# A tile of its own for each evicted query-key piece, and the staging of meta values on the tiles of the head outputs

## The chip, the cores and the metric

One core of one Trainium2 chip. The metric is the device time of one execution in microseconds (us). Instructions run on five engines, each in the order of its own program: TensorE (PE, with its weight loads as PEld), VectorE (DVE), ScalarE (ACT), GpSimd (POOL) and SyncE (SP), which issues most transfers (DMA). An engine that waits holds up all that stands behind it in its own program.

## The reference

One block of a streaming encoder, for 16 meta tokens and 1024 frames of width 1024. Both attention branches take a common input projection; one is softmax attention with a forget term, the other is stick-breaking attention.

```python
xn = rms_norm(h, norm_gains[layer, 0])
proj = xn @ w_in[layer]
q_a, k_a, v_a, f_a, q_b, k_b, v_b, g_a, g_b = jnp.split(proj, SPLIT_POINTS, axis=-1)
log_f = jax.nn.log_sigmoid((f_a + b_forget[layer]).astype(jnp.float32))
o_a = forgetting_attention(_split_heads(q_a, N_HEADS_FOX), ..., log_f.transpose(0, 2, 1))
o_b = stick_breaking_attention(_split_heads(q_b, N_HEADS_SB), ...)
mixed = (jax.nn.sigmoid(g_a) * (o_a @ w_o_fox) + jax.nn.sigmoid(g_b) * (o_b @ w_o_sb)) @ w_out[layer]
h = h + rms_norm(mixed, norm_gains[layer, 1])
xn = rms_norm(h, norm_gains[layer, 2])
u = causal_depthwise_conv(xn @ w_up[layer], conv_w[layer], conv_b[layer])
ffn = (gelu(u_gate) * u_val) @ w_down[layer]
h = h + rms_norm(ffn, norm_gains[layer, 3])
```

The forget branch computes softmax(q k / 8 + c[t] - c[s]), where c is the running sum of log_f. The stick-breaking branch computes sigmoid(z[t,s]) times the product of (1 - sigmoid(z[t,j])) for s < j < t. Eight heads of 64 in each branch, in blocks of 128 queries.

## The kernel before

Every product is made of three: each operand is split into a rounded high part and a low part, and high x high, high x low and low x high are added up in one PSUM bank (`products`, L133). The 1040 token columns are cut into three pieces, PCS = 272, 384 and 384 columns, so that a piece fits a bank.

**The heads.** Heads run as x = 0 to 15: branch b=0 (forget) heads 0 to 7, then b=1 (stick-breaking) heads 0 to 7. For one head, `qk_head` projects q and k together: 24 matmuls for a piece into a "lin" bank of pool `pl` (2 banks, L339 `pq`), evicted by VectorE into `qkt` (L343). ScalarE copies it to the high parts (L345, L347) and GpSimd, or VectorE in b=1 from head 2 on, subtracts the low parts (L90, into q2 and kb). `v_pair` does the values of two heads: `pv` in the same "lin" banks, evicted into `vt` (one buffer, L301), transposed (`vtr`, L309), and split into vv. The 16 meta values are transposed by themselves (`vtm`, L314), copied by ScalarE to a small tile `vst` (L322) and sent to `vmini` by two transfers (L325). The transposes use a bank of pool psS, tag "s", in b=0, and of psT, tag "tr", in b=1.

**Attention.** Scores (L362, L363, with a mask product L365 in b=1) go to psS banks. In b=0 VectorE takes the minimum, ScalarE the exponential, VectorE the reciprocal, and GpSimd multiplies the row (L410, tile `pr`, six buffers). In b=1 ScalarE makes two sigmoids (L395, L396), VectorE a running product (L413, `kp`), GpSimd a product (L414). For each two blocks (c = 0 to 3) there follow transposes of `pr` (`tm`, L424, and `tr`, L434), a cast by ScalarE (L438) and a subtraction by VectorE (L439) into `pt`, and products with the values (`po`, L428 and L444). The lower half of `po` is copied by ScalarE to `ot` (L447, two buffers), added by VectorE into `os` (L449), and sent out.

**Banks.** psS, psT and psO have 3, 2 and 1 banks for b=0. At the end of head 7 they are closed and opened anew with 2, 3 and 1 (`psum_pools`); the new banks wait for the last readers of the old.

**What sets the order.** The program is written head by head: attention of head x, then `prep` of the next head (q, k and, every second head, v), then `gate` (L133 `pg`, evicted at L500). A scheduler in the framework orders the instructions of each engine from a simulated timeline: it puts on each engine what it takes to be ready first, in program order where all are ready, and an eviction under `high_priority` earlier. Projections (`pq`, `pv`, `pg`) so end up between the attention steps, and fill TensorE while the other engines work on a row. Which tile an instruction asks for decides what it must wait for, and with it the order.

In names such as s0772 the digits are the branch, the head, the block and the column piece; po073 is branch, head and pair of blocks, tr0731 one group of it; pq, qkt are branch, head and piece; pv, vt, vtr, vst are branch and pair of heads (with piece or group); pr076 is head and block with a leading branch digit; pg41 is gate and piece. q211 is the second-half query tile of branch 1, head 1; kb1 is one of two key tiles shared by all heads.

Of the kernel before, what the change touches and what calls it, by code (L numbers as in the profile page):

```python
# [8 lines left out]
F32 = mybir.dt.float32  # L9
# [7 lines left out]
P = 128  # L17
D = 1024
KT = 8
NM = 16  # L20
# [5 lines left out]
DH = 64  # L26
# [23 lines left out]
def block_kernel(ctx, tc, xa, xb, wqk, wv, wf, bfg, wg, wo, wout, wup, wdn, gains, conv, cst, out):  # L50
# [124 lines left out]
    with ExitStack() as pa:  # L175
# [100 lines left out]
        for i in range(2):  # L276
            t = ap1.tile([P, 256], F32R, name=f"ptm{i}")
# [12 lines left out]
        def v_pair(b, p):  # L290
            hi, lo = load_w(wv[b * 4 + p], KT * P, f"v{b}{p}", hv=True) if b or p else early["v"]()
            yield
            vt = ap1.tile([P, L], F32, tag="vt", name=f"vt{b}{p}")
            for i, (n0, n1) in enumerate(PCS):
                if b == 0 and p == 0:
                    ps = psT.tile([P, 512], F32, tag="tr", name=f"pv{b}{p}{i}")
                else:
                    ps = pl.tile([P, 512], F32, tag="lin", name=f"pv{b}{p}{i}")
                products(ps[:, : n1 - n0], hi, lo, xs[i], 0, KT, 0, n1 - n0)
                with tc.high_priority(offset=200):  # L300
                    nc.vector.tensor_tensor(vt[:, n0:n1], ps[:, : n1 - n0], rs1[:, n0:n1], op=ALU.mult)  # L301
                yield
            vps, vtag = (psT, "tr") if b else (psS, "s")
            vv = ap2.tile([P, 8, 2, 2, DH], F32R, tag="vv", name=f"vv{b}{p}")
            for g in range(2):
                pt = vps.tile([P, 4, 2, DH], F32, tag=vtag, name=f"vtr{b}{p}{g}")
                for j in range(4):
                    c0 = NM + (4 * g + j) * P
                    nc.tensor.transpose(pt[:, j, :, :].rearrange("p a b -> p (a b)"), vt[:, c0 : c0 + P], ident)  # L309
                hv = vv[:, 4 * g : 4 * g + 4, :, 0, :]  # L310
                nc.scalar.copy(hv, pt)
                nc.vector.tensor_tensor(vv[:, 4 * g : 4 * g + 4, :, 1, :], pt, f(hv), op=ALU.subtract)
            pt = vps.tile([P, 4, 2, DH], F32, tag=vtag, name=f"vtm{b}{p}")
            nc.tensor.transpose(pt[0:NM, 0, :, :].rearrange("p a b -> p (a b)"), vt[:, 0:NM], ident)  # L314
            vm = vms[p % 2]
            src = pt[0:NM, 0, :, :]
            nc.scalar.copy(vm[0:NM, :, 0, :], src)
            nc.scalar.copy(vm[32:48, :, 0, :], src)
            nc.vector.tensor_tensor(vm[0:NM, :, 1, :], src, f(vm[0:NM, :, 0, :]), op=ALU.subtract)
            nc.vector.tensor_tensor(vm[32:48, :, 1, :], src, f(vm[0:NM, :, 0, :]), op=ALU.subtract)  # L320
            st = ap2.tile([NM, 2, DH], F32, tag="vst", bufs=1, name=f"vst{b}{p}")
            nc.scalar.copy(st, src)  # L322
            for hh in range(2):
                h = 2 * p + hh
                nc.sync.dma_start(vmini[b][NM * h : NM * (h + 1), :], st[:, hh, :])  # L325
            yield vv, vm

        def qk_head(b, h):
            hi, lo = load_w(wqk[b * NH + h], KT * P, f"qk{b}{h}", nc.vector if b and h > 1 else None, hv=not (b and h > 1)) if b or h else early["qk"]()
            yield  # L330
            q2 = ap2.tile([P, L], F32R, tag="q2", name=f"q2{b}{h}")
            k1 = ap2.tile([P, L], F32R, tag="k1", name=f"k1{b}{h}")
            k2 = kb[h % 2]
            if b == 1 and h < 2:
                nc.vector.memset(f(k2[DH:P, :]), 0.0)
            low = nc.vector if b and h > 1 else nc.gpsimd
            for i, (n0, n1) in enumerate(PCS):
                ps = pl.tile([P, 512], F32, tag="lin", name=f"pq{b}{h}{i}")
                w = n1 - n0  # L339
                products(ps[:, :w], hi, lo, xs[i], 0, KT, 0, w)  # L340
                t = ap2.tile([P, 384], F32, tag="qkt", name=f"qkt{b}{h}{i}")[:, :w]
                with tc.high_priority(offset=200):
                    nc.vector.scalar_tensor_tensor(t, ps[:, :w], qsc[:, b : b + 1], rs1[:, n0:n1],  # L343
                                                   op0=ALU.mult, op1=ALU.mult)
                nc.scalar.copy(q2[0:DH, n0:n1], t[0:DH])  # L345
                sub(low, q2[DH:P, n0:n1], t[0:DH], q2[0:DH, n0:n1])
                nc.scalar.copy(k1[DH:P, n0:n1], t[DH:P])  # L347
                sub(low, k2[0:DH, n0:n1], t[DH:P], k1[DH:P, n0:n1])
                yield
            nc.sync.dma_start(f(k1[0:DH, :]), f(k1[DH:P, :]))  # L350
            if b == 0:
                if h:
                    nc.sync.dma_start(f(k2[64:66, :]), cd[h])
                q1 = qb[h % 2]
                nc.sync.dma_start(f(q1[0:DH, :]), f(q2[0:DH, :]))
                yield q2, k1, q1[0:66, :], k2[0:66, :]
            else:
                yield q2, k1, q2, k2
# [755 lines left out]
```

## Time and profile before

| | |
|---|---|
| time, median of 3 runs | 1648.77 us (1648.71 to 1649.92) |
| the profiled execution's own time | 1648.93 us |
| its span | 1647.1 us |
| mean clock granted to TensorE | 0.998 |
| TensorE busy | 1623.7 us (99%) |
| VectorE, ScalarE, GpSimd busy | 1096.3, 830.5, 375.5 us |

The span is what the trace covers; 1.8 us of the execution lie around it. The next lines are the page's first engine rows by slices of the span, 40 equal slices of 41 us each, in tenths (9 is 90% or more).

```profile
PE   8999999999999999999999999999999999999997
DVE  7456566666788878655536887888888877333532
ACT  6354445444666766544345554565555556333420
POOL 1365656556243333403201000000000000000001
PEclk9999999999999999999999999999999999999999
```

Attention and its projections fill the slices from the second to about the eighteenth; then come the output projections and the gated merge, the up-projection, the convolution and the down-projection.

### The profile page before, as it was taken

Reading aid. Unit: us, or ns where it says so; the run is one execution under the profiler, and the core shown is the slowest. Engines: PE = TensorE matmul, PEld = TensorE weight load, DVE = VectorE, ACT = ScalarE, POOL = GpSimd, SP = SyncE. Lnnn points to the kernel's source line nnn. Section 1 sums busy time; section 2 is a strip of 40 time slices with the busy share of each in tenths; the row PEclk is TensorE's granted clock in tenths of the full one; section 3 lists DMA queues with packets and bytes.
Section 4 is the critical chain, followed back from the end, with each engine's and each line's share of the span. In section 5 each row is a group of like instructions: output and inputs, shape, how many; then the busy total and the mean of one; then the engine's idle time right before and its main releaser. Section 6 shows DMA issues by size and latency. Waiting matters only on the chain.

```text
span 1647.1 us, 29715 instructions
## 1 busy us (share of the span) xinstructions
PE 1623.7 (99%) x11672; PEld 1572.0 (95%) x11672; DVE 1096.3 (67%) x1874; ACT 830.5 (50%) x1712; POOL 375.5 (23%) x264
## 2 busy tenths in 40 slices
PE   8999999999999999999999999999999999999997
PEld 7999999999999999999999999999999999888887
DVE  7456566666788878655536887888888877333532
ACT  6354445444666766544345554565555556333420
POOL 1365656556243333403201000000000000000001
PEclk9999999999999999999999999999999999999999
DMA  4312121212111111274343552223332236445552
GB/s 183 85 57 72 54 63 51 75 39 72 46 48 41 40 32 62 73 208 146 125 129 114 170 172 85 97 90 108 97 99 97 78 109 204 140 145 150 175 183 77
DMA packets 77788, 168.48 MB, mean 102 GB/s; under 512 B 10288, under 2 KB 33584, under 8 KB 77648
## 3 DMA queue, kind: packets, MB, share of 16 engines
q1 hardware_dynamic: 77104, 166.06, 32.0%
q8 instruction: 92, 1.51, 0.4%
q10 hardware_dynamic: 544, 0.52, 0.1%
q14 instruction: 48, 0.39, 0.1%
HBM read 124.85 MB, written 35.24 MB: 97 GB/s over the span
## 4 chain that ended last, share of the span: by engine, by line
PE 95%; issue 2%; ACT 1%; DVE 1%; DMA 1%; SPq 0%; POOL 0%; DVEq 0%; POOLq 0%; ACTq 0%
PE pd L945 15%; PE A L815 13%; PE pq L133 11%; PE pg L133 10%; PE B L815 7%; PE pm L638 6%; PE pv L133 6%; PE pu L638 5%; PE y L133 5%; PE po L444 4%; PE tr L434 4%; PE R L815 3%; PE s L363 2%; PE s L362 2%; PE tm L424 1%
## 5 line engine op out<-in xcount | busy, mean ns | idle before, releaser
L945 PE MATMUL pd<-g,wh_d 128*128 128x512 f32 x616 | 191.5, 392 | 0.0
L994 POOL TENSOR_TENSOR acc<-acc,hr 128x512 f32<-128x512 f32 x4 | 5.0, 1274 | 720.8 <-DVE acc L987 720.8
L745 DVE SCALAR_TENSOR_TENSOR c<-us,cb,c 128x512 f32<-128x512 f32 x176 | 129.7, 748 | 32.9 <-ACT c L743 31.9
L945 PEld LDWEIGHTS pd<-g,wh_d 128*128 128x128 f32 x616 | 115.3, 188 | 25.0
L410 POOL TENSOR_SCALAR pr<-pr,mx 128x144 f32<-128x144 f32 (+3 forms) x64 | 114.5, 1794 | 106.2 <-DVE mx L409 56.7
L414 POOL TENSOR_TENSOR pr<-pr,kp 128x143 f32<-128x143 f32 (+3 forms) x64 | 84.7, 1328 | 168.1 <-DVE kp L413 106.4
L439 DVE TENSOR_TENSOR pt<-tr,pt 128x512 fp32r<-128x512 f32 (+1 forms) x160 | 98.8, 633 | 33.7 <-ACT pt L438 31.1
L945 PE MATMUL pd<-g,wl_d 128*128 128x512 f32 x308 | 120.8, 392 | 0.0
L444 PE MATMUL po<-pt,vv 128*128 128x256 f32 (+1 forms) x640 | 110.1, 280 | 0.0
L438 ACT CAST pt<-tr 128x512 fp32r<-128x512 f32 (+1 forms) x160 | 83.7, 542 | 51.9 <-PE tr L434 49.3
L90 DVE TENSOR_TENSOR wl_d<-wr_d,wh_d 128x896 fp32r<-128x896 f32 (+1 forms) x42 | 47.7, 1136 | 89.7 <-ACT wh_d L121 89.5
L413 DVE TENSOR_TENSOR_SCAN kp<-kp 128x144 f32<-128x144 f32 (+3 forms) x64 | 95.1, 1492 | 11.9 <-ACT kp L395 11.3
L444 PEld LDWEIGHTS po<-pt,vv 128*128 128x128 f32 x640 | 94.2, 189 | 0.2
L403 ACT ACTIVATE pr<-s,mx 128x144 f32<-128x144 f32 (+6 forms) x112 | 59.7, 539 | 67.2 <-DVE mx L401 52.2
L434 PE MATMUL tr<-cs,pr 128*128 128x128 f32 x576 | 92.7, 274 | 0.0
L121 ACT CAST wh_d<-wr_d 128x896 fp32r<-128x896 f32 (+1 forms) x42 | 41.2, 980 | 88.7 <-PE pd L945 84.0
L743 ACT ACTIVATE c<-us,cb 128x512 f32<-128x512 f32 x88 | 71.0, 815 | 21.1 <-DMA gdr<-c 15.1
L362 PE MATMUL s<-k,q 128*128 128x264 f32 (+9 forms) x240 | 79.2, 332 | 0.0
L133 PE MATMUL pg<-xh,wh_g 128*128 128x384 f32 (+1 forms) x384 | 74.8, 324 | 1.6 <-DVE qkt L343 1.4
L133 PE MATMUL pq<-xh,wh_qk 128*128 128x272 f32 (+1 forms) x360 | 74.5, 327 | 0.0
L133 PE MATMUL y<-o,wh_o 128*128 128x258 f32 x512 | 73.0, 284 | 1.1 <-ACT o L575 0.9
L133 PE MATMUL pg<-xh,wl_g 128*128 128x384 f32 (+1 forms) x384 | 73.9, 322 | 0.0
(300 smaller groups left out, 4484.7 us busy)
## 6 DMA issues: line engine op xcount, KB each, us to landing
wu<-in_wup SPq DMA_DIRECT2D x40, 512.0 KB, 3.6
wr_d<-in_wdn SPq DMA_DIRECT2D x28, 448.0 KB, 3.9
gdr<-c SPq DMA_DIRECT2D x44, 256.0 KB, 3.8
gr<-gdr SPq DMA_DIRECT2D x44, 256.0 KB, 4.2
gs<-gd SPq DMA_DIRECT2D x16, 513.0 KB, 4.2
wr_g<-in_wg SPq DMA_DIRECT2D x16, 512.0 KB, 3.6
wr_wo<-in_wout SPq DMA_DIRECT2D x16, 512.0 KB, 3.4
wr_qk<-in_wqk SPq DMA_DIRECT2D x15, 512.0 KB, 5.1
```

What stands on the lines that cost most here:

```text
L133: marks["mm"] = nc.tensor.matmul(ps, w[:, k * P : (k + 1) * P], x[:, k - k0, n0:n1], start=(k == k0 and s == 0), stop=(k == k1 - 1 and s = ...
L362: nc.tensor.matmul(ps[:tn, :n], q2[:, t0 : t0 + tn], k1[:, s0:s1], start=True, stop=False)
L410: nc.gpsimd.tensor_scalar(pr[:, :w], pr[:, :w], z, None, op0=ALU.mult)
L413: nc.vector.tensor_tensor_scan(r, r, r, 1.0, op0=ALU.mult, op1=ALU.bypass)
L414: nc.gpsimd.tensor_tensor(pr[:, : w - 1], pr[:, : w - 1], kp[:, 1:w], op=ALU.mult)
L434: nc.tensor.transpose(tr[:, x * P : (x + 1) * P], prs[tb][:, NM + j * P : NM + (j + 1) * P], ident)
L439: nc.vector.tensor_tensor(pt[:, 1, :n], tr[:, :n], f(pt[:, 0, :n]), op=ALU.subtract)
L444: nc.tensor.matmul(po[:, o0:256], vj, pt[:, s, 256 * j : min(256 * j + 256, n)], start=False, stop=(last and j == 1 and s == 1))
L638: nc.tensor.matmul(ps, (hi, hi, lo)[s][:, c : c + P], xs[kh][s == 1][:, k, :], start=(s == 0 and kh == 0 and k == 0), stop=(s == 2 and kh ...
L745: nc.vector.scalar_tensor_tensor(c, u[:, :, tap : tap + 256], cb[:, x, tap : tap + 1], c, op0=ALU.mult, op1=ALU.add)
L815: nc.tensor.matmul(ps, w[:, (k0 + i) * P : (k0 + i + 1) * P], x[:, i, :], start=(first and s == 0 and i == 0), stop=(s == 2 and i == 3), s ...
L945: nc.tensor.matmul(ps, a[:, (k - k0) * P : (k - k0 + 1) * P], x[:, c0:c1], start=(k == 0 and s == 0), stop=(k == NK - 1 and s == 2))
```

## The change

It does two things. The eviction tile `qkt` was one tag with two buffers of 384 columns, through which a head's three pieces rotated. Now the first piece has a tag of its own ("qk0", one buffer of 272 columns), and the other two pieces share a tag with two buffers, so that each piece of a head has its own tile. The staging tile `vst` had a buffer of its own in pool ap2. Now it is taken from pool apl under tag "ot", whose two buffers also take the lower halves of the head outputs. Per partition of SBUF the first part takes 1088 bytes more and the second 512 less.

```diff
@@ v_pair
-            st = ap2.tile([NM, 2, DH], F32, tag="vst", bufs=1, name=f"vst{b}{p}")
+            st = apl.tile([NM, 2, DH], F32, tag="ot", name=f"vst{b}{p}")
             nc.scalar.copy(st, src)
@@ qk_head
                 products(ps[:, :w], hi, lo, xs[i], 0, KT, 0, w)
-                t = ap2.tile([P, 384], F32, tag="qkt", name=f"qkt{b}{h}{i}")[:, :w]
+                t = ap2.tile([P, w], F32, tag="qkt" if i else "qk0", bufs=2 if i else 1, name=f"qkt{b}{h}{i}")
```

No instruction is added or removed. The order changes on all engines, from the first head to the end of attention, and is the same from there on. Three places follow.

**TensorE at the border from b=0 to b=1.** From the last scores of head (0,7); pg40 is the first piece of gate 4. Before:

```order
L362 MATMUL s0772_4517<-k107_4089,q207_4088 128x344
L363 MATMUL s0772_4517<-kb1_151,qb1_152 128x344
L133 MATMUL pg40_5296<-xh0_114,wh_g4_5292 128x258 x8
L133 MATMUL pg40_5296<-xl0_115,wh_g4_5292 128x258 x8
L133 MATMUL pg40_5296<-xh0_114,wl_g4_5293 128x258
L444 MATMUL po071_4374<-pt0710_4386,vv03_3578 128x256
L133 MATMUL pg40_5296<-xh0_114,wl_g4_5293 128x258 x5
L444 MATMUL po071_4374<-pt0710_4386,vv03_3578 128x256 x3
L444 MATMUL po071_4374<-pt0711_4397,vv03_3578 128x256
L424 MATMUL tm072_4444<-cs_74,pr074_4409 16x128
L424 MATMUL tm072_4444<-cs_74,pr075_4426 16x128
```

After the change:

```order
L362 MATMUL s0772_4517<-k107_4089,q207_4088 128x344
L363 MATMUL s0772_4517<-kb1_151,qb1_152 128x344
L444 MATMUL po071_4374<-pt0710_4386,vv03_3578 128x256 x4
L444 MATMUL po071_4374<-pt0711_4397,vv03_3578 128x256
L424 MATMUL tm072_4444<-cs_74,pr074_4409 16x128
L424 MATMUL tm072_4444<-cs_74,pr075_4426 16x128
L444 MATMUL po071_4374<-pt0711_4397,vv03_3578 128x256
L444 MATMUL po071_4374<-pt0711_4397,vv03_3578 128x128 x2
L434 MATMUL tr0720_4450<-cs_74,pr074_4409 128x128
L434 MATMUL tr0720_4450<-cs_74,pr075_4426 128x128
L434 MATMUL tr0720_4450<-cs_74,pr074_4409 128x128
L434 MATMUL tr0720_4450<-cs_74,pr075_4426 128x128
```

The projections pg40, pg41, pg42, pv110 and pv111, 120 matmuls, now stand ahead of s0772; from it to the first matmul of pv112 there are only rows of attention and the transposes vtr10 and vtm10.

**GpSimd in the same place.** From the normalisation of block 6 of head (0,7) on (wl_v11 is the low part of a weight tile). Before:

```order
L410 TENSOR_SCALAR pr076_4490<-pr076_4490,mx76_4491 128x912
L90 TENSOR_TENSOR wl_v11_5658<-wr_v11_5655,wh_v11_5657 128x1024
L90 TENSOR_TENSOR q211_5193<-qkt110_5221,q211_5193 64x272
L90 TENSOR_TENSOR kb1_151<-qkt110_5221,k111_5194 64x272
L90 TENSOR_TENSOR q211_5193<-qkt111_5252,q211_5193 64x384
L90 TENSOR_TENSOR kb1_151<-qkt111_5252,k111_5194 64x384
L410 TENSOR_SCALAR pr077_4507<-pr077_4507,mx77_4508 128x1040
L90 TENSOR_TENSOR q211_5193<-qkt112_5283,q211_5193 64x384
L90 TENSOR_TENSOR kb1_151<-qkt112_5283,k111_5194 64x384
```

After the change, from the row behind pr075 on:

```order
L90 TENSOR_TENSOR q211_5193<-qkt110_5221,q211_5193 64x272
L90 TENSOR_TENSOR kb1_151<-qkt110_5221,k111_5194 64x272
L410 TENSOR_SCALAR pr076_4490<-pr076_4490,mx76_4491 128x912
L90 TENSOR_TENSOR q211_5193<-qkt111_5252,q211_5193 64x384
L90 TENSOR_TENSOR kb1_151<-qkt111_5252,k111_5194 64x384
L90 TENSOR_TENSOR q211_5193<-qkt112_5283,q211_5193 64x384
L90 TENSOR_TENSOR kb1_151<-qkt112_5283,k111_5194 64x384
L410 TENSOR_SCALAR pr077_4507<-pr077_4507,mx77_4508 128x1040
L414 TENSOR_TENSOR pr100_4910<-pr100_4910,kp00_4911 128x143
```

wl_v11 has moved up, ahead of pr070, and all six subtractions of head (1,1) now stand ahead of pr077, two of them also ahead of pr076.

**VectorE at the end of head (1,5).** The third eviction of the last head, qkt172; kp57 is the running product over the last block of head 5. Before:

```order
L439 TENSOR_TENSOR pt1522_7285<-tr1522_7281,pt1522_7285 128x384
L90 TENSOR_TENSOR kb1_151<-qkt170_7913,k117_7887 64x272
L90 TENSOR_TENSOR kb1_151<-qkt171_7944,k117_7887 64x384
L90 TENSOR_TENSOR q217_7886<-qkt170_7913,q217_7886 64x272
L413 SCALAR_TENSOR_TENSOR kp57_7313<-kp57_7313 128x1040
L343 SCALAR_TENSOR_TENSOR qkt172_7975<-pq172_7950,qsc_77,rs1_113 128x384
L500 TENSOR_TENSOR gst120_8493<-pg120_8468,rs1_113 128x258
L90 TENSOR_TENSOR q217_7886<-qkt171_7944,q217_7886 64x384
L413 SCALAR_TENSOR_TENSOR kp60_7604<-kp60_7604 128x144
L449 TENSOR_TENSOR os152_7294<-po152_7250,ot152_7292 64x256
L90 TENSOR_TENSOR q217_7886<-qkt172_7975,q217_7886 64x384
```

After the change:

```order
L439 TENSOR_TENSOR pt1521_7274<-tr1521_7269,pt1521_7274 128x512
L343 SCALAR_TENSOR_TENSOR qkt172_7975<-pq172_7950,qsc_77,rs1_113 128x384
L439 TENSOR_TENSOR pt1522_7285<-tr1522_7281,pt1522_7285 128x384
L90 TENSOR_TENSOR kb1_151<-qkt170_7913,k117_7887 64x272
L90 TENSOR_TENSOR kb1_151<-qkt171_7944,k117_7887 64x384
L90 TENSOR_TENSOR kb1_151<-qkt172_7975,k117_7887 64x384
L90 TENSOR_TENSOR q217_7886<-qkt170_7913,q217_7886 64x272
L413 SCALAR_TENSOR_TENSOR kp57_7313<-kp57_7313 128x1040
L90 TENSOR_TENSOR q217_7886<-qkt171_7944,q217_7886 64x384
L90 TENSOR_TENSOR q217_7886<-qkt172_7975,q217_7886 64x384
L413 SCALAR_TENSOR_TENSOR kp60_7604<-kp60_7604 128x144
```

qkt172 has moved from behind kp57 and three subtractions to a place before pt1522, ahead of all of them.

## The prediction

> **What bounds the kernel now.** I read the page first (busy time by engine, then the chain that ended last), then what TensorE waited for, then the time line at each place where the new order differs.
>
> ```profile
> span 1647.1 us, 29715 instructions
> PE 1623.7 (99%) x11672; PEld 1572.0 (95%) x11672; DVE 1096.3 (67%) x1874; ACT 830.5 (50%) x1712; POOL 375.5 (23%) x264
> PE 95%; issue 2%; ACT 1%; DVE 1%; DMA 1%; SPq 0%; POOL 0%; DVEq 0%; POOLq 0%; ACTq 0%
> PE pv L133 <- ACT whi_v L105: 6.7, 2, 5.6
> PE s L363 <- DMA kb<-cd: 1.4, 1, 1.4
> PE pg L133 <- DVE qkt L343: 1.4, 1, 1.4
> PE pv L133 <- DVE vt L301: 0.8, 2, 0.5
> PE vtr L309 <- DVE vt L301: 0.3, 1, 0.3
> ```
>
> TensorE is busy 99% of the span and holds 95% of the chain. It is idle 1647.1 - 1623.7 = 23.4 us, and the longest waits are the first weights (6.7 us), which the change does not touch. So a changed order cannot win more than a few us, but it can lose many: the instruction set is the same in both programs, and whatever idle time the new order makes on TensorE is added to the time in full. The question is where, in the new order, TensorE has only work whose inputs are not there yet.
>
> **What the change removes.** With one tile for each of a head's three pieces, the eviction qkt (L343) no longer waits for the readers of the piece before last. The trace has one TensorE wait of that kind:
>
> ```profile
> 621.70 1.65 PE L133 MATMUL pg<-xh,wh_g 128*128 128x384 f32 x8 [1.37 <-DVE qkt L343]
> 623.20 1.55 PE L133 MATMUL pg<-xl,wh_g 128*128 128x384 f32 x8
> 624.58 1.55 PE L133 MATMUL pg<-xh,wl_g 128*128 128x384 f32 x8
> ```
>
> The third piece of the last head stood behind a scan and three subtractions on VectorE; now it stands ahead of them. The projection bank comes free early, and 1.4 us go (1.37 at most, since 1.37 is all that was waited; nothing else on TensorE waits for that bank in this stretch). Call it -1.4.
>
> The order at the start of attention changes too. The first-head product of s with kb (L363) waits 1.38 us for the forget row, which comes from HBM at the end of a long chain.
>
> ```profile
> 77.05 0.69 PE L363 MATMUL s<-kb,qb 66*128 66x144 f32 x3 [1.38 <-DMA kb<-cd]
> 77.83 1.55 PE L133 MATMUL pv<-xh,wh_v 128*128 128x384 f32 x8
> 79.22 1.55 PE L133 MATMUL pv<-xl,wh_v 128*128 128x384 f32 x8
> ```
>
> Eight matmuls of 384 columns go at 79.22 - 77.83 = 1.39 us, 0.174 each. In the new order 18 more projection matmuls (2 of 272 and 16 of 384 columns, 2 x 0.125 + 16 x 0.174 = 3.0 us) stand before that product, but the forget products that begin the chain stand 9 matmuls later (1.6 us), and a weight cast and an eviction go ahead inside the chain on VectorE (the neighbours of this kind take some 0.6 us each). The wait becomes 1.38 + 1.6 - 3.0 = 0 to 1.2 us; I take 0.4: -1.0 (bounds -1.4 and 0). The 0.3 us of vtr behind vt also goes, because the first vtr moved behind other matmuls: -0.3 (bounds -0.3 and 0).
>
> **What the change moves.** The copy of the meta values (vst, L322) now asks for an "ot" tile, two of which rotate through all head outputs. It therefore comes after the outputs of the head before; in the order on ScalarE vst01 is behind ot013, some 15 rows later.
>
> ```profile
> L322 ACT COPY vst<-vtm x8: 238/255/256, 47.7 to 640.5; 16x128 f32<-16x128 f32 x8
> DMA to landing us min/median/max: 1.7/1.7/1.8
> ```
>
> The copy itself is a quarter of a us, and its two transfers land 1.7 us after they are issued; the output after next (ot021 for vst01) now waits for them, but comes several us later, so I cost that at nothing, and at 1.5 each if the cover were gone. Until vst is done it holds the score bank in which vtm lies (in b=0 that is tag "s"). Scores come later, projections earlier, and this adds up: by head 7 of b=0 its attention stands 18 us of TensorE work later than before, with the projections that used to lie between it already spent. As long as there is work to do that costs nothing. It is given back at one place, the border from b=0 to b=1.
>
> ```profile
> 401.24 0.32 PE L363 MATMUL s<-kb,qb 66*128 66x344 f32 x1
> 401.40 1.11 PE L133 MATMUL pg<-xh,wh_g 128*128 128x258 f32 x8
> 432.78 0.91 PE L133 MATMUL pv<-xh,wh_v 128*128 128x384 f32 x4
> 401.56:432.78 31.22, 31.22 (x230) 30.94 (x228) 21.64 (x37) 20.72 (x50) 16.22 (x14) 1.00 0.21 67
> 13.38 1.85 PE L133 MATMUL pv<-xh,wlo_v 128*128 128x272 f32 x8
> 16.56 1.16 PE L133 MATMUL pq<-xh,wlo_qk 128*128 128x272 f32 x8
> ```
>
> The stretch from the last score of head (0,7) (s0772, ends at 401.56) to the third piece of pv11 (432.78) is 31.22 us, and TensorE (second number) is never idle in it. By the order of before it holds 120 projection matmuls: 24 of 258 columns (0.119 each, since the 8 last 1.11 us in all and the last of them 0.28), 72 of 384 (0.174), and 24 of 272 (0.125, in the same way from the 1.16 of the row at 16.56). That is 2.9 + 12.5 + 3.0 = 18.4 us. The other 12.8 us are attention. In the new order all 120 stand ahead of s0772, and none is left between it and pv112. No other can be put there: pv110 and pv111 hold both projection banks until VectorE evicts them into vt, a single tile still read by vtr10 and vtm10, and those need banks that open when the outputs of head (0,7) are done. So the chain below is bare, with 12.8 us of TensorE work inside it:
>
> ```profile
> 398.60 2.56 POOL L410 TENSOR_SCALAR pr<-pr,mx 128x912 f32<-128x912 f32 x1 [5.28 <-DVE mx L409]
> 401.14 2.40 POOL L90 TENSOR_TENSOR wl_v<-wr_v,wh_v 128x1024 fp32r<-128x1024 f32 x1
> 403.61 0.77 POOL L90 TENSOR_TENSOR q<-qkt,q 64x272 fp32r<-64x272 f32 x1
> 404.46 0.76 POOL L90 TENSOR_TENSOR kb<-qkt,k 64x272 fp32r<-64x272 f32 x1
> 405.30 1.00 POOL L90 TENSOR_TENSOR q<-qkt,q 64x384 fp32r<-64x384 f32 x1
> 407.75 2.92 POOL L410 TENSOR_SCALAR pr<-pr,mx 128x1040 f32<-128x1040 f32 x1 [0.37 <-ACT ot L447]
> 401.44 0.42 ACT L345 CAST q<-qkt 64x272 fp32r<-64x272 f32 x1
> ```
>
> GpSimd. The subtractions into q211 and kb1 write buffers that s0772 reads, so they start when it ends, after ScalarE's first copy (0.42, with a hand-off 0.7). In the new order the last normalisation (pr077, 2.92) comes behind two small ones, pr076 and four larger ones: 0.7 + 0.77 + 0.76 + 2.56 + 4 x 1.00 + 2.92 = 11.7, and six gaps of 0.08 (403.61 + 0.77 to 404.46) make 12.2; I say **12.4**. In before pr077 was done at 410.67, 9.1 us after s0772, under cover.
>
> From there to pv112 the work is transposes, casts, subtractions and products of four rounds, then vtr, vtm, and the eviction of vt. The nearest row is the same passage at the end of head (1,3), almost without idle time:
>
> ```profile
> 556.42 0.27 PE L424 MATMUL tm<-cs,pr 128*16 128x128 f32 x1
> 557.90 1.61 PE L133 MATMUL pv<-xh,wl_v 128*128 128x384 f32 x8
> 565.42 0.81 PE L133 MATMUL pv<-xh,wh_v 128*128 128x384 f32 x3 [0.32 <-DVE vt L301]
> 556.96 1.61 DVE L413 TENSOR_TENSOR_SCAN kp<-kp 128x272 f32<-128x272 f32 x2
> 416.31 0.99 DVE L413 TENSOR_TENSOR_SCAN kp<-kp 128x400 f32<-128x400 f32 x1 [0.16 <-ACT kp L395]
> 421.10 1.25 DVE L413 TENSOR_TENSOR_SCAN kp<-kp 128x528 f32<-128x528 f32 x1
> 424.12 1.52 DVE L413 TENSOR_TENSOR_SCAN kp<-kp 128x656 f32<-128x656 f32 x1 [0.72 <-ACT kp L395]
> 429.54 1.79 DVE L413 TENSOR_TENSOR_SCAN kp<-kp 128x784 f32<-128x784 f32 x1 [3.44 <-ACT kp L395]
> 418.28 0.69 DVE L439 TENSOR_TENSOR pt<-tr,pt 128x512 fp32r<-128x512 f32 x1 [0.20 <-ACT pt L438]
> 431.25 0.39 DVE L449 TENSOR_TENSOR os<-po,ot 64x256 f32<-64x256 f32 x1
> 431.56 0.42 DVE L301 TENSOR_TENSOR vt<-pv,rs 128x272 f32<-128x272 f32 x1
> ```
>
> There, tm133 to pv132 takes 565.42 - 556.42 = 9.0 us. Here VectorE has four scans in the passage (0.99 + 1.25 + 1.52 + 1.79 = 5.55), four subtractions (at most 2.8), and three evictions of about 0.4: 9.5 us, and with four hand-offs of some 0.4 at most 11.2. So pv112 starts 12.4 + 9.0 = 21.4 to 23.6 us after s0772, with 12.8 us of work for it: idle 8.6 to 10.8, I take **+9.7**. The wider bounds are 5 (GpSimd's small pieces done before s0772 and pr077 4 us sooner) and 13 (VectorE and GpSimd in each other's way).
>
> The wait is in order on TensorE, so all later work is late by the same amount; behind pv112 both orders have done the same work, and nothing later waits long enough to hand it back (pv behind vt, 0.8 in all).
>
> At the end of head (1,3) itself eight pv131 matmuls (8 x 0.174 = 1.4) moved from behind tm133 to ahead of it, and scores and transposes of 0.7 moved in: 0.32 of wait becomes 0.32 + 1.4 - 0.7 = 1.0. By the order the score s1420 is also 2.6 us later, so up to two scans (1.61) get in the way. That is +0.7 to +2.3, or less if vt is early: I take **+1.3** (bounds 0.3 and 2.5).
>
> **The sum:** -1.4 - 1.0 - 0.3 + 9.7 + 1.3 = +8.3. The profiled execution took 1648.93 us (1.8 around its span), within 0.2 of the median of 1648.77, so 1648.93 + 8.3 = **1657.2**. With the inner bounds of the terms the sum gives 1655.1 to 1660.6, with the wider ones 1651.1 to 1663.0.
>
> **Rivals.**
> First, **the border is covered** and the time is not slower. If the chain after s0772 took no more than the 12.8 us of attention that lie in it, the order would cost nothing there: -1.4 - 1.0 - 0.3 + 1.3 = -1.4, or 1647.5 (1646.1 without the loss in head (1,3)). Up to a chain of 12.8 + 1.4 + 3.3 = 17.5 the result would still be no difference. For it speaks that TensorE was never idle in the 31.22 us of before; against it that 18.4 of those were projections, that pr077 took 9.1 us even then, and that the passage behind it takes 9.0 where almost nothing is idle. Chance 0.17, with 0.05 of it for a time faster by over 0.2%, which would need gains that no wait here offers.
>
> Second, **TensorE runs slowly after the stall.** At the start eight matmuls of 272 columns lasted 1.85 us, three us later 1.16, so they were slower by 59% without any wait. After the 1.37 us gap at 621.70 the next eight took 1.50 (623.20 - 621.70) and the next 1.38, so such a gap does not do it. If the border made 6 us of work run at the early pace, 6 x 0.59 = 3.5 more: 1660.7. My pieces of idle time are under 2 us each, with work between; chance 0.11. The Trainium skill, "TensorE: Matmul & The Clock Gate", section "What's actually happening", says that the array falls to half its clock after an idle window of about 3.4 us and needs as long a busy one to return; one such window would be an estimated 3.4 us more here, none if the pieces of idle time stay as short as I think. The slow start agrees with that rule; no row shows a fall in mid-run.
>
> Third, **more places lose**: banks and POOL work moved in the earlier heads too, and two to four waits of the size of those above (1.4 to 1.7) would add 3 to 7: 1660 to 1664. The trace has no such wait in b=0 after the first head, and the order leaves projections ahead of every bank there; 0.12.
>
> That **the change does nothing** is out: the evictions' waits are gone in the order, and qkt172 moved ahead of the scan. The forecast has the rest, 0.60.
>
> **How the numbers follow.** What a measurement of this kernel can tell from no change is about 0.2%, 3.3 us, so no difference reaches to 1652.1. Slower: 0.60 + 0.11 + 0.12 = 0.83, less 0.05 for the low end of the forecast (1651.1) = 0.78; same 0.12 + 0.05 = 0.17; faster 0.05. The range must take in the forecast's bounds and the first rival's 1646.1 (cases of 0.17): 1646 to 1664. The upper end is the third rival's. The likeliest case alone has 1651 to 1663.
>
> **What would show it.** Right: a TensorE idle time of 8 to 11 us in all between s0772 and pv112, about 20 us later than the 401 of before, released by transposes' evictions, by pr on GpSimd and, last, by vt on VectorE; pr077 ending some 12 us after s0772; no wait of pg for qkt; less than 1.2 us behind kb<-cd; about 1 us more at pv132. Wrong: TensorE busy in that stretch (first rival), or matmuls of 384 columns at over 0.25 us behind it (second), or idle time of over 1 us in heads 1 to 6 of b=0 (third).

## The result and the profile after

The changed kernel takes **1671.22 us** (median of 4 runs, 1668.63 to 1672.59) against 1648.74 before (4 runs, 1648.54 to 1649.92): ratio 1.0131, 95% interval 1.0118 to 1.0143. It is slower, as forecast, but by 22.5 us and not by 8.3, and outside the range that ended at 1664.

The page of the changed kernel, its span and its busy times, and then what TensorE waited for (engine, line, what it waited on; us in total, times, longest):

```profile
span 1669.8 us, 29694 instructions
PE 1633.4 (98%) x11672; PEld 1577.8 (94%) x11672; DVE 1096.5 (66%) x1874; ACT 829.1 (50%) x1712; POOL 374.2 (22%) x264
PE pv L133 <- ACT whi_v L105: 7.9, 2, 5.7
PE po L444 <- DVE pt L439: 4.5, 7, 1.3
PE pv L133 <- DVE gst L500: 1.8, 1, 1.8
PE po L428 <- DVE ptm L427: 1.8, 3, 0.8
PE po L444 <- ACT pt L438: 1.6, 2, 1.4
PE tr L434 <- DVE ptm L427: 1.4, 1, 1.4
PE pg L133 <- DVE gst L500: 1.4, 1, 1.4
PE pv L133 <- DVE vt L301: 0.9, 1, 0.9
```

The span grew by 22.7 us with the same 11672 matmuls. TensorE's busy time grew by 9.7 (1633.4 less 1623.7), its idle time by 13.0. So part of the loss is waits and part is the same matmuls taking longer. The wait of pg behind qkt (1.37) is gone, as forecast, and so is that of s behind kb<-cd (1.38), of which the forecast left 0.4. In their place stand many waits of the attention products, for the casts and subtractions just ahead of them.

Three stretches of the time line hold most of the loss. The columns are the stretch, its length and, for each engine, busy us and instructions; then TensorE's granted clock, the share of the DMA engines and GB/s. The changed kernel, then the kernel before:

```profile
245.00:260.00 15.00, 12.73 (x78) 11.76 (x77) 7.50 (x20) 10.50 (x27) 10.99 (x8) 0.89 0.17 42
330.00:350.00 20.00, 17.80 (x117) 16.48 (x117) 11.49 (x31) 12.81 (x34) 14.01 (x11) 1.00 0.25 65
425.00:460.00 35.00, 28.90 (x181) 25.89 (x180) 28.29 (x47) 25.06 (x64) 17.73 (x15) 0.90 0.09 18
```

```profile
245.00:260.00 15.00, 15.00 (x108) 14.87 (x107) 9.29 (x27) 6.83 (x23) 5.65 (x5) 1.00 0.13 41
330.00:350.00 20.00, 20.00 (x140) 19.89 (x140) 12.34 (x34) 8.61 (x25) 9.32 (x7) 1.00 0.14 44
425.00:460.00 35.00, 35.00 (x252) 34.46 (x251) 27.54 (x41) 21.82 (x56) 10.63 (x8) 1.00 0.08 24
```

Before, TensorE was busy without a gap in all three. After, it idles 2.3, 2.2 and 6.1 us, and in the first and the third its clock is down. The third is the border that the prediction spoke of. The first two are the ends of heads (0,3) and (0,5), of which it did not.

How late each kernel runs can be read off at equal work. For each matmul I take its start in the trace, less the time that the matmuls ahead of it in its order need at full pace; this lateness, less that of the kernel before at the same amount of work, is what was lost so far. The table gives what was lost in each stretch of work (us), up to 825 us of work, where attention and gates are long over; the four columns on the right are runs told of below. Full pace is read from the usual distance between matmuls of a shape; read a little higher or lower, it moves some tenths of a us between neighbouring rows, and leaves the sums as they are.

| stretch, TensorE work done | forecast | change | change again | pieces only | staging only | hold three |
|---|---|---|---|---|---|---|
| 0 to 225: start, heads (0,0) to (0,2) | -1.3 | +0.7 | -1.3 | -1.0 | -0.1 | +1.8 |
| 225 to 250: end of (0,3) | 0 | +4.5 | +3.4 | -0.2 | 0.0 | +0.8 |
| 300 to 325: end of (0,5) | 0 | +3.7 | +3.7 | 0.0 | -0.1 | 0.0 |
| 375 to 425: border | +9.7 | +12.3 | +12.4 | +6.2 | +3.6 | +1.7 |
| 450 to 475: end of (1,1) | 0 | +1.2 | +1.2 | +1.2 | +0.9 | +1.2 |
| 525 to 550: end of (1,3) | +1.3 | +1.2 | +1.2 | +1.2 | +1.0 | +1.2 |
| 575 to 600: pg behind qkt | -1.4 | -1.7 | -1.7 | -1.7 | -1.3 | -1.7 |
| 675 to 725: last gates, start of the output projection | 0 | +2.6 | +1.0 | +2.2 | -0.2 | +1.6 |
| all the rest | 0 | -1.5 | -1.5 | -1.6 | -0.2 | +1.5 |
| sum | +8.3 | +23.0 | +18.4 | +6.3 | +3.6 | +8.1 |

### The profile page after: what moved, and what is told of

The parts are those of the page before. It is cut to its first block, busy times and chain, and to the rows that moved or that the text cites. A ratio compares the mean times of both kernels' runs of the same rounds, so it can differ in the third digit from the quotient of the medians.

```text
span 1669.8 us, 29694 instructions
## 1 busy us (share of the span) xinstructions
PE 1633.4 (98%) x11672; PEld 1577.8 (94%) x11672; DVE 1096.5 (66%) x1874; ACT 829.1 (50%) x1712; POOL 374.2 (22%) x264
## 4 chain that ended last, share of the span: by engine, by line
PE 91%; DVE 3%; ACT 2%; DMA 2%; issue 1%; POOL 0%; SPq 0%; DVEq 0%; POOLq 0%; ACTq 0%
PE pd L945 15%; PE A L815 13%; PE pq L133 10%; PE pg L133 9%; PE B L815 6%; PE pm L638 6%; PE pv L133 5%; PE pu L638 5%; PE y L133 5%; PE po L444 4%; PE tr L434 3%; PE R L815 3%; PE s L362 2%; PE s L363 2%; DVE kp L413 1%; PE tm L424 1%
## 5 line engine op out<-in xcount | busy, mean ns | idle before, releaser
L444 PE MATMUL po<-pt,vv 128*128 128x256 f32 (+1 forms) x640 | 115.1, 286 | 6.2 <-DVE pt L439 4.5
L133 PE MATMUL pg<-xl,wh_g 128*128 128x384 f32 (+1 forms) x384 | 76.7, 324 | 0.0
```

The costliest lines, as they stand in the source:

```text
L133: marks["mm"] = nc.tensor.matmul(ps, w[:, k * P : (k + 1) * P], x[:, k - k0, n0:n1], start=(k == k0 and s == 0), stop=(k == k1 - 1 and s = ...
L444: nc.tensor.matmul(po[:, o0:256], vj, pt[:, s, 256 * j : min(256 * j + 256, n)], start=False, stop=(last and j == 1 and s == 1))
```

## The border

The changed kernel in the time line of TensorE and of GpSimd: start, us, engine, line, tiles, and in brackets the wait just before:

```profile
428.88 0.32 PE L363 MATMUL s<-kb,qb 66*128 66x344 f32 x1
432.45 0.56 PE L444 MATMUL po<-pt,vv 128*128 128x256 f32 x3 [1.32 <-DVE pt L439]
436.38 0.47 PE L365 MATMUL s<-smask 128*128 128x128 f32 x1 [1.14 <-DVE smask L549]
453.09 1.65 PE L133 MATMUL pv<-xh,wh_v 128*128 128x384 f32 x8 [0.92 <-DVE vt L301]
431.54 2.56 POOL L410 TENSOR_SCALAR pr<-pr,mx 128x912 f32<-128x912 f32 x1
438.49 2.92 POOL L410 TENSOR_SCALAR pr<-pr,mx 128x1040 f32<-128x1040 f32 x1
```

s0772 ends at 429.20, and pr077 is done at 438.49 + 2.92 = 441.41, 12.2 us later (12.4 forecast). pv112 starts at 453.09, 23.9 us after s0772 (21.4 to 23.6 forecast), and waits for vt, as named. With 12.2 us of work in the passage by its order (12.8 in the forecast) it loses 11.7; the term was +9.7.

Two things differ from the forecast. TensorE is idle for only 6.1 us of the passage, where 8 to 11 were named as the sign; the other 5.7 us are its own matmuls taking longer than at full pace, some at half rate (clock 0.50 from 433.3 to 440.1) and some one by one. And no wait for pr is booked on TensorE. Its transpose of pr077 starts at 441.57, 0.16 us after GpSimd is done, right behind work of its own. That work was late as well, behind the mask of the new branch: smask_raw is asked for at 432.90, and its cast on VectorE ends at 436.3 (the wait of 1.14 above). The chain that the profile follows back goes over ScalarE's copies and this load, and not over GpSimd. So two chains end together there, and which of them sets the first half of the passage is not shown.

## The experiments

Four theories. **A**: the loss is projections that run ahead of attention and are then missing, so that attention stands bare. **B**: the pieces part alone makes it; three pieces evicted early put six copies in a row on ScalarE, ahead of the casts. **C**: the staging part alone makes it, by holding a score bank. **D**: the tiles themselves make it, whatever the order.

### One part at a time

Only the pieces (with one tile shared by the two uses of `mini`, which frees 512 bytes per partition; in the run below that has the same sharing, the order on TensorE is that of before up to 619 us):

```diff
-                t = ap2.tile([P, 384], F32, tag="qkt", ...)[:, :w]
+                t = ap2.tile([P, w], F32, tag="qkt" if i else "qk0", bufs=2 if i else 1, ...)
-            w = ap1.tile([2, NH, NM], F32, name=f"mw{b}")
+            w = ap1.tile([2, NH, NM], F32, tag="mw", name=f"mw{b}")
```

> Only the part with a tile for each piece; vst keeps its own buffer (512 bytes per partition come from sharing one small tile between the two uses of mini, which leaves the order as it was). Theory A, projections run ahead of attention and are missing later: in the order of this kernel one bare stretch of attention is left in b=0, 10.8 us of TensorE work at the border (13.8 with both parts; 5.4 and 3.9 more in heads 3 and 5 with both, none of those here), and 7.4 instead of 5.3 in heads (1,1) and (1,3). s0772 to pv112 holds 18.6 us of work here, and the passage took 23.9 with both parts: about 5 us idle at the border, 1 to 3 us in b=1, 1 to 3 in the gates, less 1.4 for pg behind qkt: 1654 to 1660. Theory B, this part alone makes the loss, since three evictions at once set six copies on ScalarE ahead of the casts: 1668 to 1672. Theory C, the vst part makes it: 1646 to 1649.

Only the staging:

```diff
-            st = ap2.tile([NM, 2, DH], F32, tag="vst", bufs=1, name=f"vst{b}{p}")
+            st = apl.tile([NM, 2, DH], F32, tag="ot", name=f"vst{b}{p}")
```

> Only the part with vst on the tiles of the head outputs; qkt as before. Theory A: one bare stretch at the border of 7.1 us, s0772 to pv112 holds 22.5 us of work against a passage of up to 23.9: 0 to 2 us idle there, 1 to 3 in heads (1,1) and (1,3), 0 to 2 in the gates: 1650 to 1655. Theory B (the pieces make the whole loss): 1648 to 1650. Theory C (vst makes it, by holding a score bank): 1668 to 1672.

Measured: pieces alone 1655.00 us (ratio 1.0038, 1.0025 to 1.0052), staging alone 1652.32 (1.0019, 1.0010 to 1.0028), with 1649.06 before. Both lie where A put them; B and C, that one part alone makes the whole loss, fall. The parts are far from adding up: 5.9 and 3.3 us apart, 22.5 together.

Why they don't add up is seen in the passages themselves. At the ends of heads (0,3), (0,5) and (0,7) the chain from the last score of the head to the third piece of the second-next pv is the same kind: casts, subtractions, products, transposes of vt, eviction of vt, with both projection banks held until then. The table gives its length in the trace, and in brackets the TensorE work that the order puts in it (us).

| passage | before | pieces only | staging only | both | both, hold three |
|---|---|---|---|---|---|
| s0372 to pv032 | 21.4 (21.3) | 10.0 (10.1) | 17.6 (17.6) | 7.9 (3.4) | 18.9 (18.7) |
| s0572 to pv102 | 28.9 (28.6) | 10.1 (10.1) | 17.5 (17.5) | 6.5 (3.1) | 29.6 (29.6) |
| s0772 to pv112 | 31.2 (30.7) | 24.5 (18.6) | 25.7 (22.2) | 23.9 (12.2) | 34.3 (32.1) |

At (0,3) and (0,5) a passage takes the work in it or the length of its chain, some 7 us, whichever is longer. At the border it takes some 24 us even with 18.6 or 22.2 us of work in it, since that work does not reach to its end: from the transpose of pr077 to pv112 it takes 11.6 us with the pieces only, 10.5 with the staging only and 11.5 with both. With one part TensorE comes to that transpose 2.3 and 3.3 us after GpSimd is done, so there GpSimd held nothing up. Each part alone uses up 4 to 18 us of the cover and still leaves (0,3) and (0,5) more work than the chain; both together leave 3.4 and 3.1. The end of the border is uncovered by either part alone. The two rows of the time line of TensorE that bound it, pieces only and then staging only:

```profile
412.03 0.32 PE L363 MATMUL s<-kb,qb 66*128 66x344 f32 x1
436.89 0.79 PE L133 MATMUL pv<-xh,wh_v 128*128 128x384 f32 x3 [0.78 <-DVE vt L301]
```

```profile
410.59 0.32 PE L363 MATMUL s<-kb,qb 66*128 66x344 f32 x1
436.64 0.62 PE L133 MATMUL pv<-xh,wh_v 128*128 128x384 f32 x2 [0.78 <-DVE vt L301]
```

What B named is real as part of the chain. At the end of (0,3) in the changed kernel ScalarE does six copies in a row before the cast that TensorE waits for:

```profile
248.47 0.42 ACT L345 CAST q<-qkt 64x272 fp32r<-64x272 f32 x1
248.91 0.42 ACT L347 CAST k<-qkt 64x272 fp32r<-64x272 f32 x1
249.35 0.51 ACT L345 CAST q<-qkt 64x384 fp32r<-64x384 f32 x1
249.89 0.51 ACT L347 CAST k<-qkt 64x384 fp32r<-64x384 f32 x1
250.42 0.51 ACT L345 CAST q<-qkt 64x384 fp32r<-64x384 f32 x1
250.96 0.51 ACT L347 CAST k<-qkt 64x384 fp32r<-64x384 f32 x1
251.49 0.58 ACT L438 CAST pt<-tr 128x512 fp32r<-128x512 f32 x1
```

```profile
252.13 0.39 PE L444 MATMUL po<-pt,vv 128*128 128x256 f32 x1 [1.44 <-ACT pt L438]
256.36 0.96 PE L133 MATMUL pv<-xh,wh_v 128*128 128x384 f32 x4
```

They write buffers that s0372 still reads, so they all come due when it ends. With projections to do, that costs TensorE nothing.

### The cover given back, with the same tiles

Both parts, and the last third of some pv piece held, in the order alone, behind the last scores of the head before. First for every pair of heads, with the second and with the first piece:

```diff
-            nc.tensor.matmul(ps[:tn, :n], q1[:, t0 : t0 + tn], k2[:, s0:s1], start=False, stop=True)
+            marks["s"] = nc.tensor.matmul(ps[:tn, :n], q1[:, t0 : t0 + tn], k2[:, s0:s1], start=False, stop=True)
-                products(ps[:, : n1 - n0], hi, lo, xs[i], 0, KT, 0, n1 - n0)
+                products(ps[:, : n1 - n0], hi, lo, xs[i], 0, KT, 0, n1 - n0, (None, None, marks.get("s") if i == 1 else None))
```

> Both parts of the change, with one rule of order more and no other tile: the last third (8 matmuls, low part of the weights) of the second piece of pv is held behind the last scores of the head before. Theory A (the loss is nothing but projections that ran ahead and are missing later): by its order no stretch of attention over 3.1 us of TensorE work stands bare, s0772 to pv112 holds 36 us of work, so the waits of heads 3 and 5 and of the border go, with the half-rate stretches behind them, and what the change won at pg behind qkt stays: 1645 to 1651. Theory D (the tiles themselves make it: ot waiting for the transfers of vst, evictions and copies of three pieces at once, which are the same here): 1664 to 1672.

> The same with the last third of the first piece of pv held in that way. Longest bare stretch 3.1 us, in (1,1). Theory A: 1645 to 1651, and close to the run with piece 1 held. Theory D: 1664 to 1672.

Measured: 1681.28 (ratio 1.0193, 1.0176 to 1.0210) and 1678.02 (1.0179, 1.0163 to 1.0194). Both expectations were missed, A's by 30 and 27 us and D's too. The traces show why the total says little here. At the places that A spoke of it holds. With the second piece held TensorE is busy throughout all three windows from above. With the first piece held nothing is lost at (0,3) and (0,5), and 0.8 at the border. TensorE is busy throughout the third window (first row), but it loses 7 us in heads (0,0) to (0,2), and then waits 16.8 us at one place in the last gates (second row):

```profile
425.00:460.00 35.00, 35.00 (x253) 34.55 (x253) 27.06 (x39) 21.93 (x55) 11.72 (x9) 1.00 0.12 39
742.37 2.93 PE L133 MATMUL pg<-xh,wh_g 128*128 128x384 f32 x8 [16.84 <-DVE gst L500]
```

There the gates' evictions stand on VectorE behind work on the outputs of attention that waits for its loads. The rule had pulled attention ahead in all sixteen heads and left more gates to the end; that is a new loss of its own, and not one of the change.

So the rule was cut to the three pairs in question, and to the third piece:

```diff
+ ..., (None, None, marks.get("s") if b * 4 + p in (2, 3, 4) and i == 2 else None))
```

> Both parts of the change with their tiles; the only rule more is that the last third of the third piece of pv is held behind the last scores of the head before, for the three pairs of heads that follow heads (0,3), (0,5) and (0,7). By its order the stretches in heads 3 and 5 are bare no more, one of 4.2 us is left at the border (13.8 in the change), and s0772 stands at 376.6 us of TensorE work (378.0 before, 396.5 in the change); from there on the order is that of the change. Theory A (projections used up early): against the kernel before, nothing in heads 3 and 5, 0 to 2 at the border, and as in the changed kernel 1.2 in (1,1), 1.2 in (1,3), -1.7 at pg behind qkt, 2.4 in the gates, -1 to +1 in the first head: 1650 to 1654. Theory D (the tiles themselves, copies of three pieces at once on ScalarE): 1664 to 1672.

Measured: 1657.84 us (1.0053, 1.0038 to 1.0068), 1649.01 before. D falls. The three places lose 0.8, 0.0 and 1.7 us instead of 4.5, 3.7 and 12.3, so 18 of the 20.5 us there were order and not tiles. The windows of this kernel at (0,3), (0,5) and the border:

```profile
245.00:260.00 15.00, 15.00 (x110) 14.81 (x109) 8.61 (x22) 5.00 (x13) 7.42 (x5) 1.00 0.19 54
330.00:350.00 20.00, 20.00 (x139) 19.91 (x139) 10.86 (x29) 6.76 (x21) 8.75 (x6) 1.00 0.16 57
420.00:445.00 25.00, 24.06 (x164) 23.18 (x163) 16.82 (x22) 14.31 (x33) 5.73 (x6) 1.00 0.16 49
```

The total is 4 us above what A expected, since the rule brought small waits of its own in heads (0,2) to (0,7): six of 0.1 to 0.65 us, and 4.7 us of lateness in all before the border.

The same for the pieces part alone, with the first piece of pv10 held:

```diff
+ ..., (None, None, marks.get("s") if b and not p and i == 0 else None))
```

> The pieces part alone with the last third of the first piece of pv10 held behind the last scores of head (0,7). Bare stretch at the border 4.3 us (10.8 without the rule). Theory A: the 5.8 us that the run without the rule lost at the border shrink to 0 to 2, all else as there: 1649 to 1652. Theory D: 1655 as without the rule.

Measured: 1656.86 (1.0054, 1.0037 to 1.0071), not less than the 1655.00 without the rule, and outside of what A gave. At the border the loss between 400 and 425 us of work went from 5.8 to 1.7 as expected, but the 100 us of work ahead of it, which had won 0.2 without the rule, lost 5.5 around new waits for pr, qkt and ptm (1.6 us idle in four of them). Holding one thing back moves the hole; it is filled only where there is work to spare.

### A second buffer for vt

Both parts, vt with two buffers and pr with five instead of six for the space:

```diff
-            vt = ap1.tile([P, L], F32, tag="vt", name=f"vt{b}{p}")
+            vt = ap1.tile([P, L], F32, tag="vt", bufs=2, name=f"vt{b}{p}")
```

> Both parts, with two buffers of vt (and five of pr for the space). The projections of v no longer wait in both banks for vt. Theory A: the places at the ends of heads 3 and 5 are bare no more, but the projections run further ahead and are missing where the next tile runs out; its order has bare stretches of 6.7, 3.9, 11.0, 6.9 and 8.5 us at other places (before pq072, pq112, pq132, pq152, pq172). So it is still slower than before by 8 to 20 us: 1657 to 1669. If the single vt alone were the cause: 1646 to 1651.

Measured: 1697.27 us (1.0294, 1.0274 to 1.0315), worse than A's bound. (0,3) and (0,5) lose nothing at their old places (TensorE 15.00 of 15.00 in the first row), and the holes stand elsewhere, in heads (0,4) and (0,6), and in b=1:

```profile
245.00:260.00 15.00, 15.00 (x107) 14.91 (x106) 8.47 (x23) 9.44 (x24) 10.55 (x8) 1.00 0.25 57
290.00:312.00 22.00, 19.82 (x104) 17.68 (x103) 12.59 (x40) 12.51 (x36) 13.95 (x11) 0.77 0.17 47
385.00:405.00 20.00, 17.31 (x99) 15.72 (x98) 11.70 (x34) 10.02 (x29) 13.75 (x9) 0.91 0.10 24
440.00:490.00 50.00, 42.65 (x295) 40.05 (x294) 37.82 (x60) 33.78 (x87) 24.14 (x18) 1.00 0.15 41
```

With a second vt the old places run dry no more, and others do, so the single vt alone does not explain the loss. How much of the new loss, 26 us above the change, is the missing sixth pr buffer was not tried apart.

### The same kernel again

> The changed kernel again, for a second trace. If TensorE's half rate after idle time depends on where the idle time falls against something that runs freely, the idle times stand at the same places (73.8, 250 to 253, 339 to 344, 430 to 453) and the half-rate stretches behind them not at all of the same: behind some that had one before there is none, or the other way; time between 1668 and 1673. If the length of the idle time decides, the half-rate stretches are those of the first trace.

Measured: 1668.07 us. Through attention the waits stand at the same places with the same sizes to 0.05 us, and one of 0.2 is new. Of the half-rate stretches only that of the border came again. The windows of the first execution at the first head, and of the second at the first head, (0,3), (0,5) and the border (the clock is the third number from the end):

```profile
60.00:80.00 20.00, 18.16 (x110) 17.84 (x109) 10.64 (x12) 7.96 (x8) 7.14 (x4) 0.91 0.31 87
```

```profile
60.00:80.00 20.00, 18.17 (x119) 17.85 (x118) 10.73 (x14) 7.96 (x8) 7.16 (x4) 1.00 0.32 90
245.00:260.00 15.00, 12.51 (x88) 11.59 (x87) 8.12 (x21) 9.51 (x23) 13.17 (x9) 1.00 0.19 46
330.00:350.00 20.00, 17.80 (x122) 16.45 (x121) 10.97 (x29) 11.59 (x29) 14.21 (x10) 1.00 0.19 55
425.00:460.00 35.00, 28.88 (x183) 25.95 (x182) 27.57 (x44) 25.66 (x65) 18.76 (x15) 0.90 0.12 31
```

In the first execution the clock also fell at the first head (0.91) and at (0,3) (0.89). The two executions differ by 3.4 us of span. The half rate makes 1.6 of it at the first head and 1.1 at (0,3). The rest is not the clock alone: 0.4 at the start and 1.6 at the last gates, less 1.3 for a wait in the down-projection that the second execution has and the first has not.

### The part that pays, alone

The kernel before with a tile of its own for the first piece of head (1,7) alone, and the one tile shared by the two uses of `mini`, as above:

```diff
-                t = ap2.tile([P, 384], F32, tag="qkt", ...)[:, :w]
+                t = ap2.tile([P, w], F32, tag="qk0", bufs=1, name="qkt170") if (b, h, i) == (1, NH - 1, 0) else ap2.tile([P, 384], F32, tag="qkt", ...)[:, :w]
```

> The kernel before, with a tile of its own for the first piece of the last head alone (1,7). The order is that of before up to that head, so no projections run ahead earlier. If the gain that the change was credited with is real, the wait of 1.37 us of pg behind qkt at 621.7 goes and nothing else moves: 1647.4 (ratio 0.9992). If something behind it, at the start of the gates, is late anyway: 1648.8.

> The kernel before with a tile of its own for the first piece of head (1,7) alone, once more, since its first ratio of 0.9988 (0.9979 to 0.9997) lies near what can be told from no change. If the gain of 1.4 us is real, again 0.998 to 1.000 with the middle below 1; if it was chance, a middle at or above 1.

Measured: ratio 0.9988 (0.9979 to 0.9997; 1647.33 us against 1649.06) and 0.9992 (0.9983 to 1.0002; 1647.90 against 1649.00). The wait for qkt is gone from both traces, and the medians are 1.7 and 1.1 us lower. The two intervals together speak for a gain of about 0.1%, but the second includes none. In both traces the lateness falls by 1.7 between 575 and 600 us of work, and 1.2 to 1.6 come back at the first output projection, where y waits 1.6 us for o instead of 0.9 and the clock is down behind it. It is the only version here whose median is below that of both kernels.

### One more gate in b=1

```diff
-LATE = 7
+LATE = 6
```

> The kernel before with LATE = 6: one more gate (72 matmuls, some 11 us of TensorE work) is given to the heads of b=1 and one less to the end of attention. Theory A: the bare stretches of 5.3 us in heads (1,1) and (1,3) are filled, so the waits there (0.2, 0.5 and 0.3 us) go, and less is left for the passage at the end, where 1.4 + 0.9 us of waits stand: 1646 to 1650. Theory B and C say nothing of it.

Measured: 1652.18 us (1.0019, 1.0010 to 1.0028), outside of what was expected. By some 475 us of work 2.0 us were won, 1.9 of them lost again at a new wait in (1,3) (tr behind ptm, 1.8), and the work missing at the end of attention cost some 5 (y waits 4.3 us for o, and TensorE slows behind it).

## Why the prediction was wrong

The direction was right, and so was the kind of loss: attention that stands bare because its projections are spent. The count of places was wrong, and so was the part of the change that was held to move the order.

- **"It is given back at one place, the border from b=0 to b=1."** This is the step that failed. The passage that I priced at the border (last score, vtr, vt, third piece of pv) ends every second head, and in the changed order it is bare at (0,3) and (0,5) too: 3.4 and 3.1 us of work for chains of 7.9 and 6.5. That is 8.2 us that the sum did not have: 4.5 of them idle (the first two windows above), the rest half rate at (0,3) and products that run one by one instead of overlapped. The order shown ahead of the result had it in it; I looked for bare attention only where the shift was greatest, and gave further places 0.12 with the words that projections stood ahead of every bank there. Shown by the traces, by the two parts apart and by holding three pieces back.
- **"What the change moves"** was put down to the staging alone, and the pieces were priced as a gain (-1.4). The pieces alone cost 5.9 us, more than the staging alone (3.3), and take more cover from all three passages. That the staging shifts the order by holding a score bank was not tried.
- **The border, +9.7:** right in place, in the moment at which pr077 is done and in the last releaser, vt. The passage took 23.9 us, a little above the upper value of 23.6; with less work in it than counted and what just precedes it, the place lost 12.3. That the wait for GpSimd sets the first half was not shown: the mask, which the step did not have, came as late, and half of the loss is slow matmuls and not idle time.
- **The first head, -1.3:** the waits named went, but a new one of 1.84 us came: pv waits for a bank whose gate eviction stands on VectorE behind the scan of the forget row. The step took it that the 18 matmuls moved ahead could run. Without the half rate the stretch still won 1.0 to 1.3 in two of the traces; in the profiled execution it lost 0.7.
- **pg behind qkt, -1.4:** -1.7 here, with the pieces only and with three pieces held, and in both traces with the last piece's tile alone. But with the staging only, where qkt is as before, 1.3 of it come too (the wait is 0.2 there). A kernel that is late on TensorE already can meet a shorter wait, so not all of it need be a gain of the tile.
- **The end of (1,3), +1.3:** +1.2. The same happens at (1,1), for the same moved scores, and was not counted: +1.2.
- **"Nothing later waits long enough to hand it back", and nothing new after the border:** the last gates and the start of the output projection lost 1.0 to 2.6 in the traces of the change, the pieces only and the three held pieces, and nothing in that with the staging alone.
- **The second rival, half rate after idle time**, at 0.11, came about as well: not in the place of the forecast but on top of it, at three places of b=0 in one execution and at one in the other. I had argued from a wait of 1.37 us that left the clock alone, and set that against pieces of idle time that were each under 2 us but close together. Its price of 3.4 us for one window was too high as well: the first half-rate stretch lasted 3.41 us and cost 1.6.

Together, measured less forecast in the profiled execution: +8.2 for the two places not seen, +2.6 at the border, +2.6 for the gates, +1.2 for (1,1), +2.0 for the start, -0.3 for qkt, -0.1 for (1,3) and -1.5 for the rest, which is the 14.7 between +8.3 and +23.0.

## What to carry to other kernels

When a buffer that held work back is made larger, ask what that work was covering. Here the wait was a brake that kept projections next to the stretches where attention had nothing else to run beside it; count, in the new order, the work between every two points that a fixed chain joins, and not only where the shift is greatest. Two such brakes may each be harmless to loosen and costly together, since a passage costs nothing until its cover falls below its chain.

## What the runs showed of the hardware

**TensorE falls to half rate after a wait of 1.84 us between busy stretches, and not always.** The first head in the changed kernel and in that with the pieces only: the same wait, and behind it eight matmuls of 272 columns.

```profile
73.76 1.31 PE L133 MATMUL pv<-xh,wh_v 128*128 128x272 f32 x8 [1.84 <-DVE gst L500]
74.88 2.00 PE L133 MATMUL pv<-xl,wh_v 128*128 128x272 f32 x8
```

```profile
73.69 1.27 PE L133 MATMUL pv<-xh,wh_v 128*128 128x272 f32 x8 [1.84 <-DVE gst L500]
74.80 1.16 PE L133 MATMUL pv<-xl,wh_v 128*128 128x272 f32 x8
```

After the same 1.84 us the one slows to 2.00 us for eight matmuls and stays slow until 78.4, the other runs on at 1.16. At (0,5), with 2.2 us idle in three pieces between 339 and 344, neither execution slowed; at the border, 6.1 us in all, both did. The Trainium skill, "TensorE: Matmul & The Clock Gate", section "What's actually happening", tells of a window of about 3.4 us that runs freely and does not start with the kernel. That fits a fall that comes and goes with the same wait; that a window must be idle as a whole does not fit a wait of 1.84 us between busy stretches.

The granted clock in the traces shows the same. In each trace its changes lie whole multiples of 3.41 us apart: 74.89, 78.30, 252.38, 255.80, 433.29 and 440.12 in the first execution. In the 3.41 us before each of its falls TensorE was busy for 46, 42 and 53% of the time. In the kernel with the pieces only, counted from its change at 14.86, the wait of the first head is split over two such stretches with 70 and 76% busy, and nothing falls. In the second execution, counted from its fall at 430.21, that wait lies in one with 54%, and the idle time at (0,3) is split over two with 67 and 64%; neither brought a fall. So a low share of busy time within one stretch goes with the fall. No sharp limit is shown: with two buffers of vt one fall came after 63%, and a stretch of 47% had none. The times of the changed kernel do not follow from this alone: of its four timed runs the one with the clock of 0.997 took 1670.88 us, and one with 0.995 took 1668.63.
